# Staggering the seven products of gate and up blocks, a fourth pair of split tiles, and another order of the down products

## The chip, the core and the metric

The kernel runs on one core of a Trainium2 chip. The metric is device time in microseconds (us) of one execution. Of the engines this document speaks of five: PE (TensorE, the matmuls), DVE (VectorE), ACT (ScalarE), POOL (GpSimd) and SP (SyncE, which here only issues transfers). Each works through its own queue of instructions in the order that was fixed when the program was built.

## The reference: one layer of a hybrid decoder

The input is x, 512 tokens by 2048 features in float32. One layer has a mixing half (a gated linear recurrence and an RWKV-7 style state recurrence, side by side), a feed-forward half, a gated embedding, and a final RMS norm. The change touches the feed-forward half and the few steps ahead of it:

```python
h  = h + mixed @ w_out                      # output projection of the mixing half
hn = rmsnorm(h, ln_ffn)
g  = causal_dwconv(hn @ w_gate, conv_w, conv_b)   # 6144 columns, width 3
u  = hn @ w_up                              # 6144 columns
h  = h + (gelu(g) * u) @ w_down
```

All arithmetic has to be as good as float32. (The names of weights are shortened here.)

## The kernel before, in words

**Splits.** Each float32 operand A is split into hi, a copy rounded to the format that PE multiplies fast, and lo = A - hi. A product is then three matmuls, hi by hi, hi by lo and lo by hi. ACT makes hi (line L130) and DVE makes lo (L131), 128x1024 elements at a time for weights. The split weights lie in three rotating pairs of tiles, `whi` and `wlo` (HL = 3); the function `wfill` takes the next items of one long list (`ffn_items`, in the order in which PE uses them) and starts their splits up to LOOK = 2 units ahead. An item is either raw weights to be loaded by SP (L123) or a function that makes a sum of weight blocks.

**Projection and first forms.** For m = 0 to 15 PE computes 128 features of the output projection, DVE adds them to the residual `hT[m]` (L1243), and `forms(m)` makes split operands (L143 to L147 in a helper): from m below 8 for two of the seven products, from m of 8 and above for the other five. ACT squares `hT[m]` and POOL adds the squares up into `acc` (L1251), from which the norm's factor is later worked out (L189 to L202).

**Gate and up.** 48 blocks, gate and up in turn, each 256 columns by all 2048 features, as a two by two scheme that needs seven products instead of eight: q5, p1, p4, p6, p7, p2, p3 in this order (block 0: p1, p4, p2, q5, p7, p6, p3). A product is 24 matmuls of 128x256 (L1264 to L1266, over 8 steps of k). Its weights are blocks of the weight matrix or sums of them: q5 takes g21 + g22, a DVE add (L1120); p6 adds one more block to the same tile with an accumulating transfer that POOL issues (L1132), and p3 yet another one in the same way; p7 takes g21 + g11, a DVE add in place (L1130); p1, p4 and p2 take blocks as they are. DVE combines the results (L1289 to L1295); a gate block then goes through the convolution (L1305 to L1311), an up block is multiplied with it (L1354), and every second pair of blocks is written to memory together with four differences of its parts (`spill`).

**Down.** Eleven chunks of 512 hidden features in four groups of 3, 3, 3 and 2, each group for two halves of columns b, which gives eight passes. A pass runs products i = 0 to 6 one after the other, each over the chunks of the group; one chunk of one product is a unit of 12 matmuls of 128x512 (L1369 to L1371). Operands: i = 0 takes d0 loaded as it is; i = 1 takes d0 + d1, a DVE add into a tile of its own (L1150, tiles s24 to s26; d1 lies in s21 to s23); i = 2 and i = 6 add one block each to that tile by accumulating transfers from POOL (L1158); i = 3 takes a load; i = 4 adds it to d1 in place (L1156); i = 5 takes raw weights. The hidden operands are loaded into tiles "tmp", which three buffers share, and split (`hidden`).

**What sets the order.** A scheduler orders the program by priorities and a model of costs, and fixes each engine's queue. `wfill` runs at raised priority. On a queue, an instruction that waits holds up all that stand behind it.

After the down stage the last chunk, transposes, the gated embedding and the final norm follow; they use "tmp" too.

Of the kernel before, what the change touches and what calls it, by code (L numbers as in the profile page):

```python
# [5 lines left out]
F32R = mybir.dt.float32r  # L6
# [5 lines left out]
D = 2048  # L12
# [11 lines left out]
GROUPS = [(0, 3), (3, 6), (6, 9), (9, 11)]  # L24
KORDER = [(0, 1, 4, 5, 2, 3, 6, 7), range(8)]
# [63 lines left out]
class Builder:  # L89
# [22 lines left out]
    def wfill_(self):  # L112
        nc = self.nc
        while self.wn < len(self.wq) and len(self.wt) < self.LOOK:
# [9 lines left out]
            if own:  # L124
# [979 lines left out]
    def gate_order(self, p, w):  # L1104
# [3 lines left out]
    def gate_unit(self, p, w, u):  # L1108
        nc, par = self.nc, 4 * (w % 2)
        src = lambda i, j: self.A["wgu"][2 * p + i, w, j]  # L1110
        buf = lambda n: self.t(self.bp, "x%d" % (par + n), (128, 8, 128), bufs=1)

        def load(n, i, j):
            t = buf(n)
            nc.sync.dma_start(t, src(i, j))
            return t
        first = p + w == 0
        if u == "q5":
            self.g21, self.g22, self.gs = load(0, 1, 0), load(1, 1, 1), buf(3)
            nc.vector.tensor_tensor(self.gs, self.g21, self.g22, ALU.add)  # L1120
            return self.gs
        if u == "p1":
            self.g11 = load(2, 0, 0)
            return self.g11
        if u == "p4":
            return self.g22
        if u == "p7":
            if first:
                self.g11 = load(2, 0, 0)
            nc.vector.tensor_tensor(self.g21, self.g21, self.g11, ALU.add)  # L1130
            return self.g21
        nc.gpsimd.dma_start(self.gs, src(0, 0 if u == "p6" else 1), accum_op=ALU.add)  # L1132
        return self.gs


    def down_unit(self, ch, c, b, i):
# [24 lines left out]
    def ffn_items(self):  # L1161
# [4 lines left out]
        for p in range(NF // 2):  # L1166
            for w in range(2):
                for o in self.gate_order(p, w):
                    if o == "p2" or p + w == 0 and o in direct:
                        i, j = direct[o]  # L1170
                        r.append((A["wgu"][2 * p + i, w, j], u))
                    else:
                        r.append((lambda p=p, w=w, o=o: self.gate_unit(p, w, o), u))
# [22 lines left out]
    def phase2(self):  # L1196
# [7 lines left out]
        acc = T("acc")  # L1204
# [475 lines left out]
```

## Time and profile before

| what | us |
|---|---|
| median of 3 runs (lowest, highest) | 2728.83 (2725.93, 2731.3) |
| the profiled execution, its span | 2718.62, 2716.5 |
| PE busy | 2584.5 (95%) |
| DVE busy | 1901.9 (70%) |
| ACT busy | 1241.8 (46%) |
| POOL busy | 254.6 (9%) |
| mixing half, to about | 840 |
| projection and first forms | 840 to 908 |
| gate and up, 48 blocks | 908 to 1953.6 |
| down, eight passes | 1953.6 to 2440 |
| the rest | 2440 to 2716.5 |

The profile shows one execution. PE's busy share counts matmuls from their start to a modelled end, so that a PE at 95% can still lose time between matmuls; what a stage loses is better seen from its length against the number of its matmuls times the spacing of undisturbed ones. A row of a timeline has start, duration, engine, line, operation, tiles out and in, and in brackets how long the engine stood idle before it and what ended that. A row of waits has the total, the count and the longest.

### The profile page before, as it was taken

The page shows a single profiled execution, that of the slowest core. Times are in us where ns is not written, and L with a number is a line of the kernel's source. Part 1 is how long each engine was busy: PE and PEld are TensorE (multiplying, and loading weights), DVE is VectorE, ACT ScalarE, POOL GpSimd, SP SyncE. Part 2 cuts the span into 40 slices and gives each one's busy share as a digit, 9 for nine tenths or more (in the row PEclk, how much of TensorE's full clock was granted, in tenths as well). Part 3 has the DMA queues.
Part 4 walks back from the last instruction along what each step waited for, and adds up shares of the span by engine and source line. Part 5 has one row for each costly group of instructions (what it writes and reads, how often), then busy time and mean ns, then how long its engine had stood idle before and what let it go on. Part 6 is the DMA issues. An engine that isn't in the chain of part 4 may idle for free.

```text
span 2716.5 us, 51689 instructions
## 1 busy us (share of the span) xinstructions
PE 2584.5 (95%) x21922; PEld 2257.1 (83%) x21922; DVE 1901.9 (70%) x2594; ACT 1241.8 (46%) x1743; POOL 254.6 (9%) x268
## 2 busy tenths in 40 slices
PE   9989999999999899999999999999989989999997
PEld 8867777777777799999999999999967777777887
DVE  5765776666758887777777777777766676796447
ACT  6463556545525544343444334344555343435335
POOL 0010001001222200000000000000000000000001
PEclk9989999999999899999999999999999999999999
DMA  7212222122334565666566565666677676853233
GB/s 251 90 59 72 84 82 75 60 87 87 117 107 142 173 180 162 184 176 171 153 186 177 167 187 149 172 175 182 184 198 221 154 210 156 225 147 109 93 97 105
DMA packets 131448, 394.29 MB, mean 145 GB/s; under 512 B 14480, under 2 KB 26640, under 8 KB 131216
## 3 DMA queue, kind: packets, MB, share of 16 engines
q1 hardware_dynamic: 111056, 317.58, 33.6%
q0 software_dynamic: 20160, 73.41, 16.2%
q8 instruction: 171, 2.80, 0.4%
q14 instruction: 61, 0.50, 0.1%
HBM read 354.49 MB, written 36.44 MB: 144 GB/s over the span
## 4 chain that ended last, share of the span: by engine, by line
issue 21%; PE 19%; DMA 17%; DVE 11%; ACT 3%; POOL 2%; POOLq 0%; ACTq 0%; DVEq 0%; SPq 0%
DMA x<-wgu 16%; DVE wlo L131 5%; ACT whi L130 2%; PE mm L1266 2%; PE mm L1475 2%; PE mm L1477 2%; PE mm L1476 2%; PE mm L1264 2%; PE mm L1265 2%; POOL s L1158 1%; PE mm L1370 1%; PE mm L1371 1%; PE mm L1369 1%; PE wk L1264 1%; PE wk L1265 1%
## 5 line engine op out<-in xcount | busy, mean ns | idle before, releaser
L1266 PE MATMUL mm<-s,wlo 128*128 128x256 f32 x1920 | 552.7, 288 | 35.8 <-DVE wlo L131 35.2
L130 ACT ACTIVATE whi<-x 128x1024 fp32r<-128x1024 f32 x330 | 337.3, 1053 | 528.9 <-DMA x<-wgu 254.2
L1264 PE MATMUL mm<-s,whi 128*128 128x256 f32 x1920 | 548.1, 285 | 11.0 <-ACT whi L130 9.2
L131 DVE TENSOR_TENSOR wlo<-x,whi 128x1024 fp32r<-128x1024 f32 x330 | 401.7, 1221 | 210.0 <-ACT whi L130 209.2
L1265 PE MATMUL mm<-s,whi 128*128 128x256 f32 x1920 | 546.0, 284 | 0.2 <-DVE s L144 0.2
L131 DVE TENSOR_TENSOR wlo<-wraw,whi 128x1024 fp32r<-128x1024 f32 (+1 forms) x241 | 293.0, 1216 | 196.8 <-ACT whi L130 195.2
L130 ACT ACTIVATE whi<-wraw 128x1024 fp32r<-128x1024 f32 (+1 forms) x241 | 245.7, 1020 | 372.1 <-PE mm L162 187.1
L1266 PEld LDWEIGHTS mm<-s,wlo 128*128 128x128 f32 x1920 | 370.5, 193 | 48.1 <-DVE wlo L131 47.9
L1264 PEld LDWEIGHTS mm<-s,whi 128*128 128x128 f32 x1920 | 370.8, 193 | 14.3 <-ACT whi L130 12.2
L1265 PEld LDWEIGHTS mm<-s,whi 128*128 128x128 f32 x1920 | 370.7, 193 | 0.5 <-DVE s L144 0.4
L160 PE MATMUL mm<-x,whi 128*128 128x512 f32 x832 | 333.1, 400 | 0.9 <-DVE hT L450 0.9
L164 PE MATMUL mm<-x,wlo 128*128 128x512 f32 x832 | 332.8, 400 | 0.0
L162 PE MATMUL mm<-x,whi 128*128 128x512 f32 x832 | 331.2, 398 | 0.0
L1370 PE MATMUL mm<-wlo,s 128*128 128x512 f32 x680 | 274.1, 403 | 20.2 <-DVE wlo L131 20.1
L1369 PE MATMUL mm<-whi,s 128*128 128x512 f32 x680 | 272.7, 401 | 19.6 <-ACT whi L130 19.5
L1371 PE MATMUL mm<-whi,s 128*128 128x512 f32 x680 | 270.7, 398 | 0.0
L1266 PE MATMUL wk<-s,wlo 128*128 128x256 f32 x768 | 218.2, 284 | 0.8 <-DVE wlo L131 0.8
L1264 PE MATMUL wk<-s,whi 128*128 128x256 f32 x768 | 218.1, 284 | 0.0
L1265 PE MATMUL wk<-s,whi 128*128 128x256 f32 x768 | 217.9, 284 | 0.0
L160 PEld LDWEIGHTS mm<-x,whi 128*128 128x128 f32 x832 | 157.7, 189 | 36.4 <-issue 3.0
L162 PEld LDWEIGHTS mm<-x,whi 128*128 128x128 f32 x832 | 157.6, 189 | 33.7 <-issue 1.8
L164 PEld LDWEIGHTS mm<-x,wlo 128*128 128x128 f32 x832 | 157.3, 189 | 33.9 <-issue 1.9
(524 smaller groups left out, 4521.2 us busy)
## 6 DMA issues: line engine op xcount, KB each, us to landing
x<-wgu SPq DMA_DIRECT2D x144, 512.0 KB, 5.7
x<-wgu POOLq DMA_DIRECT2D x96, 512.0 KB, 5.5
wraw<-wz SPq DMA_DIRECT2D x80, 512.0 KB, 3.5
wraw<-wgu SPq DMA_DIRECT2D x50, 512.0 KB, 5.7
x<-wd SPq DMA_DIRECT2D x44, 512.0 KB, 4.3
s<-wd POOLq DMA_DIRECT2D x44, 512.0 KB, 6.0
wraw<-wpg SPq DMA_DIRECT2D x31, 512.0 KB, 3.5
wraw<-wd SPq DMA_DIRECT2D x30, 512.0 KB, 4.4
```

The costliest lines, as they stand in the source:

```text
L130: nc.scalar.activation(hi, raw, AF.Copy)
L131: nc.vector.tensor_tensor(lo, raw, hi.bitcast(F32), ALU.subtract)
L160: nc.tensor.matmul(ps, hi[:, k, :], xh, start=first and i == 0, stop=False)
L162: nc.tensor.matmul(ps, hi[:, k, :], xl, start=False, stop=False)
L164: nc.tensor.matmul(ps, lo[:, k, :], xh, start=False, stop=last and i == n - 1)
L1264: TE.matmul(ps, wh[:, k, :], xh, start=k == 0, stop=False)
L1265: TE.matmul(ps, wh[:, k, :], xl, start=False, stop=False)
L1266: TE.matmul(ps, wl[:, k, :], xh, start=False, stop=k == 7)
L1369: TE.matmul(ps, x[0][:, k, ts_], w[0][:, k, :], start=first and k == 0, stop=False)
L1370: TE.matmul(ps, x[0][:, k, ts_], w[1][:, k, :], start=False, stop=False)
L1371: TE.matmul(ps, x[1][:, k, ts_], w[0][:, k, :], start=False, stop=last and k == 1)
L1475: TE.matmul(pg[tt], xh[:, ts_], wh[:, i, :], start=first and u + i == 0, stop=False)
```

## The change: what it does

1. **Gate order.** `gate_order` is now one list over all 48 blocks. Block n runs q5, then p3 of block n-1, then p1, p4, p6, p7, p2 of its own; p3 of the last block comes at the end. Block 0 runs p1, p4, p2, q5, p7, p6. The state of a block is kept in a dictionary, because two blocks are open at a time.
2. **Fourth pair.** Every fourth weight split (k % 4 == 3) goes into tiles x12 and x15 instead of the three rotating pairs, and LOOK is 3. The working tiles of a block that lay in x15 move into two buffers "fm", the outputs of up blocks use two tiles (x10, x11) instead of three.
3. **p6 of blocks 0 and 47** is summed by a DVE add instead of an accumulating transfer.
4. **Down order** is 1, 0, 2, 3, 6, 4, 5; the load of d0 is made with product 1, and the hidden operands are prepared in the same order.
5. **First forms.** For m of 8 and above the intermediate sums are formed with one DVE and one ACT instruction less, and DVE instead of POOL adds the squares up. `acc` lies in another pool.
6. **"tmp"** has two buffers instead of three.

```diff
+ORDER = (1, 0, 2, 3, 6, 4, 5)
...
-            if own:
+            if len(own) == 2:
+                hi, lo = (self.t(self.bp, n, shape, F32R, bufs=1) for n in own)
+            elif own:
...
-        return ("p1", "p4", "p2", "q5", "p7", "p6", "p3") if p + w == 0 else ("q5", "p1", "p4", "p6", "p7", "p2", "p3")
+        o = [(0, u) for u in ("p1", "p4", "p2", "q5", "p7", "p6")]
+        for n in range(1, NF):
+            o += [(n, "q5"), (n - 1, "p3")] + [(n, u) for u in ("p1", "p4", "p6", "p7", "p2")]
+        return o + [(NF - 1, "p3")]
...
-        nc.gpsimd.dma_start(self.gs, src(0, 0 if u == "p6" else 1), accum_op=ALU.add)
-        return self.gs
+        if u == "p6" and n in (0, NF - 1):
+            nc.vector.tensor_tensor(g["s"], g["s"], g[11], ALU.add)
+        else:
+            nc.gpsimd.dma_start(g["s"], src(0, 0 if u == "p6" else 1), accum_op=ALU.add)
+        return g["s"]
...
         if i == 0:
-            self.d0[c] = load(plain(), 0, 0)
             return self.d0[c]
         if i == 1:
-            self.d1[c], self.dq[c] = load(buf(21 + c), 0, 1), buf(24 + c)
+            self.d0[c], self.d1[c], self.dq[c] = load(plain(), 0, 0), load(buf(21 + c), 0, 1), buf(24 + c)
             nc.vector.tensor_tensor(self.dq[c], self.d0[c], self.d1[c], ALU.add)
...
+        for k, (n, o) in enumerate(self.gate_order()):
+            own = (("x12", "x15") if k % 4 == 3 else ())
...
-                for i in range(7):
+                for i in ORDER:
...
+        self.LOOK = 3
...
-            f1 = T("tmp", 3, (128, 2, 256))
-            differ(f1[:, 0], k)
+            f1 = T("fm", 2, (128, 2, 256))
             if m < 8:
+                V.tensor_tensor(f1[:, 0], b, a, ALU.subtract)
...
-            SC.activation(f1[:, 0], f1[:, 0], AF.Copy, scale=g0)
-            SC.activation(f1[:, 1], halves(hT[k])[1], AF.Copy, scale=g0)
-            V.scalar_tensor_tensor(f2[:, 0], b, g, f1[:, 0], ALU.mult, ALU.subtract)
+            SC.activation(f1[:, 0], b0, AF.Copy, scale=g0)
+            V.scalar_tensor_tensor(f1[:, 1], b, g, f1[:, 0], ALU.mult, ALU.subtract)
+            V.scalar_tensor_tensor(f2[:, 0], a0, g0, f1[:, 1], ALU.mult, ALU.add)
             V.scalar_tensor_tensor(f2[:, 1], a, g, f2[:, 0], ALU.mult, ALU.subtract)
-            V.scalar_tensor_tensor(f3[:, 0], b, g, f1[:, 1], ALU.mult, ALU.subtract)
...
-                sq = T("tmp", 3)
+                sq = T("tmp", 2)
                 SC.activation(sq, hT[m], AF.Square)
-                G.tensor_tensor(acc, acc, sq, ALU.add)
+                (G if m < 8 else V).tensor_tensor(acc, acc, sq, ALU.add)
...
-                hids[ch, i] = hidden(src, 3 * i + ch - lo)
+                hids[ch, i] = hidden(src, 3 * ORDER.index(i) + ch - lo)
...
-            for i in range(7):
+            for j, i in enumerate(ORDER):
```

How the queues move, first **DVE in a steady stretch of the gate stage**, before. The rows from the split of p3 of one block on (`wlo` from x3) to the next block's combination; L131 with a `wlo` is a lo, x3 or x7 holds the sum for q5, p6 and p3 of even or odd blocks.

```order
L1289 TENSOR_TENSOR x15_1916_13642<-wk_1925_13732,x15_1916_13642 128x256
L1290 SCALAR_TENSOR_TENSOR x15_1916_13642<-mm_1917_13643,x15_1916_13642 128x256
L131 TENSOR_TENSOR wlo_1931_13768<-x3_1906_13568,whi_1930_13767 128x1024
L1120 TENSOR_TENSOR x3_1961_14032<-x0_1959_14028,x1_1960_14030 128x1024
L1292 TENSOR_TENSOR x15_1916_13642<-x15_1916_13642,wk_1929_13765 128x256
L1130 TENSOR_TENSOR x0_1959_14028<-x0_1959_14028,x2_1964_14062 128x1024
L131 TENSOR_TENSOR wlo_1937_13805<-x7_1935_13802,whi_1936_13804 128x1024
L1293 TENSOR_TENSOR x8_1914_13640<-mm_1917_13643,x15_1916_13642 128x512
L131 TENSOR_TENSOR wlo_1940_13835<-x6_1938_13832,whi_1939_13834 128x1024
L1295 TENSOR_TENSOR x8_1914_13640<-mm_1932_13797,x15_1916_13642 128x512
```

The same stretch after the change; there the lines are L134 (lo), L1127 (add for q5), L1137 (add for p7) and L1294 to L1300 (combination), and x15 as a target is the lo of the fourth pair.

```order
L134 TENSOR_TENSOR wlo_1931_13699<-wraw_1929_13696,whi_1930_13698 128x1024
...
L134 TENSOR_TENSOR wlo_1937_13734<-x7_1935_13731,whi_1936_13733 128x1024
L1294 TENSOR_TENSOR fm_1917_13593<-wk_1932_13726,fm_1916_13592 128x256
L1295 SCALAR_TENSOR_TENSOR fm_1916_13592<-mm_1919_13595,fm_1917_13593 128x256
L134 TENSOR_TENSOR x15_1940_13766<-x3_1906_13497,x12_1939_13765 128x1024
L1127 TENSOR_TENSOR x3_1963_13963<-x0_1961_13959,x1_1962_13961 128x1024
L1297 TENSOR_TENSOR fm_1917_13593<-fm_1917_13593,wk_1938_13763 128x256
L1137 TENSOR_TENSOR x0_1961_13959<-x0_1961_13959,x2_1970_14028 128x1024
L134 TENSOR_TENSOR wlo_1944_13799<-x6_1942_13796,whi_1943_13798 128x1024
L1298 TENSOR_TENSOR x8_1918_13594<-mm_1919_13595,fm_1917_13593 128x512
```

Before, p3's lo (from x3) stands ahead of both adds of the next block and of its q5's lo (from x7). After, q5's lo of the next block (from x7) stands ahead of p3's lo (from x3), and the add for a q5 that stands behind it (L1127) is that of the block after the next one, into x3 again.

**DVE at the boundary of two down passes**, before: lo's of products 5 (from `wraw`) and 6 (s24 to s26), and the adds L1150 for the next pass.

```order
L131 TENSOR_TENSOR wlo_3178_23215<-wraw_3176_23212,whi_3177_23214 128x1024
L131 TENSOR_TENSOR wlo_3180_23232<-s24_3128_22942,whi_3179_23231 128x1024
L1150 TENSOR_TENSOR s24_3199_23345<-x0_3187_23285,s21_3198_23343 128x1024
L131 TENSOR_TENSOR wlo_3182_23249<-s25_3132_22962,whi_3181_23248 128x1024
...
L1150 TENSOR_TENSOR s25_3203_23365<-x1_3190_23303,s22_3202_23363 128x1024
L131 TENSOR_TENSOR wlo_3186_23270<-s26_3138_22986,whi_3185_23269 128x1024
...
L1150 TENSOR_TENSOR s26_3215_23404<-x2_3195_23325,s23_3214_23402 128x1024
L131 TENSOR_TENSOR wlo_3189_23288<-x0_3187_23285,whi_3188_23287 128x1024
L131 TENSOR_TENSOR wlo_3192_23306<-x1_3190_23303,whi_3191_23305 128x1024
```

After, where L1159 is that add and the lo's are those of products 4 (s21 to s23) and 5 (`wraw`):

```order
L134 TENSOR_TENSOR wlo_3209_23186<-s21_3151_22881,whi_3208_23185 128x1024
L134 TENSOR_TENSOR wlo_3211_23203<-s22_3156_22903,whi_3210_23202 128x1024
...
L1159 TENSOR_TENSOR s24_3229_23301<-x0_3227_23297,s21_3228_23299 128x1024
L134 TENSOR_TENSOR wlo_3213_23220<-s23_3161_22925,whi_3212_23219 128x1024
L1159 TENSOR_TENSOR s25_3234_23323<-x1_3232_23319,s22_3233_23321 128x1024
L134 TENSOR_TENSOR wlo_3218_23242<-wraw_3216_23239,whi_3217_23241 128x1024
L1159 TENSOR_TENSOR s26_3239_23345<-x2_3237_23341,s23_3238_23343 128x1024
L134 TENSOR_TENSOR wlo_3221_23260<-wraw_3219_23257,whi_3220_23259 128x1024
...
L134 TENSOR_TENSOR wlo_3224_23278<-wraw_3222_23275,whi_3223_23277 128x1024
L134 TENSOR_TENSOR wlo_3231_23304<-s24_3229_23301,whi_3230_23303 128x1024
```

Before, the adds stood among the lo's of product 6 and behind them came the lo's of the next pass's product 0, from plain loads x0 and x1. After, they stand among the lo's of products 4 and 5, write s24 to s26 from loads into s21 to s23, which product 4's splits just read, and the first lo's of the next pass are those of the sums.

**DVE from the gate's end into the first down pass**, before:

```order
L1292 TENSOR_TENSOR x15_2859_21670<-x15_2859_21670,wk_2902_21868 128x256
L131 TENSOR_TENSOR wlo_2914_21919<-x0_2912_21916,whi_2913_21918 128x1024
...
L1293 TENSOR_TENSOR x12_2858_21669<-mm_2860_21671,x15_2859_21670 128x512
L131 TENSOR_TENSOR wlo_2923_21964<-x1_2921_21961,whi_2922_21963 128x1024
...
L1150 TENSOR_TENSOR s24_2944_22031<-x0_2912_21916,s21_2943_22029 128x1024
...
L131 TENSOR_TENSOR wlo_2942_22014<-x2_2940_22011,whi_2941_22013 128x1024
L1150 TENSOR_TENSOR s25_2948_22051<-x1_2921_21961,s22_2947_22049 128x1024
L131 TENSOR_TENSOR wlo_2946_22034<-s24_2944_22031,whi_2945_22033 128x1024
```

After:

```order
L1295 SCALAR_TENSOR_TENSOR fm_2896_21658<-mm_2899_21661,fm_2897_21659 128x256
L1297 TENSOR_TENSOR fm_2897_21659<-fm_2897_21659,wk_2944_21897 128x256
L1298 TENSOR_TENSOR x11_2898_21660<-mm_2899_21661,fm_2897_21659 128x512
...
L1159 TENSOR_TENSOR s24_2947_21902<-x0_2945_21898,s21_2946_21900 128x1024
L1300 TENSOR_TENSOR x11_2898_21660<-mm_2956_21949,fm_2896_21658 128x512
L1159 TENSOR_TENSOR s25_2959_21954<-x1_2957_21950,s22_2958_21952 128x1024
L134 TENSOR_TENSOR wlo_2949_21905<-s24_2947_21902,whi_2948_21904 128x1024
L1159 TENSOR_TENSOR s26_2970_22003<-x2_2968_21999,s23_2969_22001 128x1024
L134 TENSOR_TENSOR wlo_2961_21957<-s25_2959_21954,whi_2960_21956 128x1024
```

Before, lo's from plain loads (x0, x1, x2) stand first and the adds between and behind them. After, two adds stand ahead of the first lo of the down stage, with the last combinations of block 47 (L1297 to L1300) in between.

More of the change, by code (lines that the diff above doesn't have):

```diff
@@ L1304, in conv @@
+            if u == "p3":
+                V.tensor_tensor(two(out[:, 0]), two(g["up"]), fm, ALU.add)
+            if n == 0 and u == "q5":
+                rt = self.tok_rstd(acc, D, RMS_EPS, k2)
+            if n == 0 and u == "p6":
+                self.rstd_bcast(acc, D, RMS_EPS, k2, rs, rt)
+            if n == NF - 1:
+                for i in {"q5": (0,), "p1": (1,), "p4": (2, 3), "p6": (4,), "p7": (5,), "p2": (6,)}.get(u, ()):
+                    group_form(0, ORDER[i])
         def conv(p, z, c):
@@ L1451, in phase2 @@
         for k in range(2):
[L1452 removed]
+            r = T("tmp", 2)
             nc.sync.dma_start(r, A["pT"][k])
```

160 lines of the change are left out of this document (74 added, 86 removed).

## The prediction, made before the changed kernel ran

> **What bounds the kernel now.** I read three views in this order: the windows by stage (how much of each stage TensorE, PE, loses), the chain of waits inside the lossy stages, and the timelines of the engines in that chain. First the windows; the columns are the window, its length, busy time and count of instructions of PE, PE's weight loads, DVE, ACT and POOL, then granted clock, DMA share and GB/s.
>
> ```profile
> 840.00:925.00 85.00, 78.86 (x364) 66.08 (x362) 81.41 (x132) 54.08 (x105) 23.47 (x15) 0.96 0.54 183
> 908.13:949.16 41.03, 30.81 (x185) 28.90 (x184) 29.88 (x43) 16.91 (x29) 9.94 (x7) 0.79 0.72 205
> 949.16:1009.64 60.48, 60.48 (x506) 60.48 (x505) 49.47 (x57) 29.23 (x31) 5.25 (x6) 1.00 0.59 161
> 1009.64:1953.60 943.96, 905.92 (x7395) 891.25 (x7394) 703.98 (x793) 384.25 (x425) 76.34 (x87) 1.00 0.62 173
> 1953.60:2027.30 73.70, 63.12 (x255) 48.56 (x254) 48.33 (x49) 36.30 (x49) 5.27 (x6) 0.95 0.75 219
> 2027.30:2440.00 412.70, 383.50 (x1612) 306.23 (x1611) 298.23 (x325) 178.12 (x209) 33.34 (x38) 0.98 0.69 185
> ```
>
> Gate blocks 1 to 3 (third row) take 60.48 us with PE never idle: 20.16 us a block of 168 matmuls, the floor. Block 0 (41.03 us) loses 20.9. The other 44 blocks need 44 x 20.16 = 887.0 and take 943.96: **56.9 us lost**. No engine is full there: DVE is busy 704 of 944 us, so what bounds is a chain. This is one turn of it:
>
> ```profile
> 1397.60 5.41 DMA x<-wgu
> 1403.05 2.77 issue
> 1405.84 6.85 DMA x<-wgu
> 1412.80 1.07 ACT whi L130
> 1413.89 1.24 DVE wlo L131
> 1415.19 1.11 issue
> 1416.29 0.41 DVE x L1292
> 1416.78 0.98 issue
> 1417.76 1.23 DVE wlo L131
> ...
> 1393.36 1.23 DVE L1120 TENSOR_TENSOR x<-x,x 128x1024 f32<-128x1024 f32 x1
> 1394.84 1.22 DVE L1130 TENSOR_TENSOR x<-x,x 128x1024 f32<-128x1024 f32 x1
> ```
>
> The accumulating transfer for p6 starts when q5's lo is out, its sum is split (the first "issue", 2.77), the transfer for p3 follows, p3 is split, and in DVE's queue p3's lo stands before the next block's L1120, L1292, L1130 and the lo of the next q5 (the last two rows show the two adds that the chain calls "issue", in the turn before). That lo starts the next p6. The turn is 5.41 + 2.77 + 6.85 + 1.07 + 1.24 + 1.11 + 0.41 + 0.98 + 1.23 and small gaps, 21.4 us against 20.16.
>
> The down stage has 154 units of 12 matmuls. The first two PE rows below are 23 matmuls apart, 0.227 us each, so 2.72 a unit and 8.17 a product of three chunks; 154 units need 419.4 us and take 73.7 + 412.7 = 486.4: **67.0 lost**. Nearly all of it stands at product i=2, whose operand is the sum of product 1 with one block of weights added by an accumulating transfer, three of them per product:
>
> ```profile
> 2169.72 0.39 PE L1369 MATMUL mm<-whi,s 128*128 128x512 f32 x1
> 2174.94 0.39 PE L1371 MATMUL mm<-whi,s 128*128 128x512 f32 x1
> 2178.52 0.50 PE L1369 MATMUL mm<-whi,s 128*128 128x512 f32 x1 [3.19 <-ACT whi L130]
> 2179.78 0.50 PE L1370 MATMUL mm<-wlo,s 128*128 128x512 f32 x1 [0.76 <-DVE wlo L131]
> 2180.97 0.63 PE L1371 MATMUL mm<-whi,s 128*128 128x512 f32 x1
> 2181.39 0.63 PE L1369 MATMUL mm<-whi,s 128*128 128x512 f32 x1
> ...
> 2162.86 0.89 POOL L1158 DMA_DIRECT2D s<-wd  x1 [30.76 <-DVE wlo L131]
> 2169.11 0.87 POOL L1158 DMA_DIRECT2D s<-wd  x1 [5.36 <-DVE s L144]
> 2177.62 0.89 POOL L1158 DMA_DIRECT2D s<-wd  x1 [7.64 <-issue]
> 2183.31 0.88 POOL L1158 DMA_DIRECT2D s<-wd  x1 [4.80 <-issue]
> 2197.62 0.87 POOL L1158 DMA_DIRECT2D s<-wd  x1 [7.50 <-DVE x L1386]
> ...
> 2231.64 0.88 POOL L1158 DMA_DIRECT2D s<-wd  x1 [33.15 <-DVE wlo L131]
> 2264.51 0.88 POOL L1158 DMA_DIRECT2D s<-wd  x1 [8.56 <-issue]
> ```
>
> Six accumulating transfers a pass (three for i=2, three for i=6) go one at a time: the six starts span 2162.86 to 2197.62, 6.95 us apart, in the next pass 2231.64 to 2264.51, 6.57 apart, 5.7 where nothing else interferes (2177.62 to 2183.31). The third start came 8.5 us after the second, and PE stood 3.19 us for that operand. Behind the gap matmuls start 0.42 apart instead of 0.227: the clock is halved for some 3.4 us, which costs about 1.7 more.
>
> The Trainium skill, "TensorE: Matmul & The Clock Gate", Part 1: The HAM clock gate, says the array falls to half clock after at least one idle window of about 3.4 us. By that, gaps below 3.4 would cost only themselves, and rival 2 below would come out 13.6 lower. The trace has the clock fall behind a gap of 3.19, so the figure is about right; for shorter gaps I keep the dearer price.
>
> **The change, part by part.** All against the profiled execution (2718.62 us, 2.1 around its span), which lies 10.2 under the median of the runs shown, 2728.83; I take savings off the median.
>
> *Gate order and fourth pair.* Work is the same count of matmuls, splits and transfers. p3 of block n moves behind q5 of block n+1, so p6 and p3 each get a product (2.88 us) more, and the lo of q5 stands ahead of p3's lo in DVE's queue: the turn above is cut open, since nothing of block n+1's q5 now waits for block n's p3. Every fourth split has a pair of its own, so a split can begin three products (8.64 us) ahead of use instead of two (5.76). From q5's lo to p3's use there is now more than a block; the chain needs 5.41 + 2.77 + 6.85 + 1.07 + 1.24 = 17.3. What remains is DVE, 704/44 = 16.0 us a block of 20.16. I expect 20.3 a block: 0.14 x 44 = 6 us lost, **51 saved** (bounds: 0.45 a block left, 37 saved; none left, 57).
>
> *Block 0 and the first forms.* The first two rows give a line's count, its shortest, median and longest duration in ns, and its first and last start.
>
> ```profile
> L147 DVE SCALAR_TENSOR_TENSOR s<-hT,par,s x22: 472/480/1526, 847.3 to 915.7; 128x256 fp32r<-128x256 f32 x22
> L1251 POOL TENSOR_TENSOR acc<-acc,tmp x10: 1420/1831/1841, 867.8 to 927.2; 128x512 f32<-128x512 f32 x10
> ...
> 904.91 0.41 DVE L1216 TENSOR_TENSOR tmp<-hT 128x256 f32<-128x256 f32 x1
> 911.01 0.41 DVE L1216 TENSOR_TENSOR tmp<-hT 128x256 f32<-128x256 f32 x1
> ```
>
> From 840 to 925 DVE is full (81.41 of 85) and one m takes it 6.1 us (904.91 to 911.01), PE 24 x 0.227 = 5.45. L147 takes 1.52 instead of 0.48 while POOL's square-sum runs. For m from 8 the change drops L1216 (0.35 in the queue), the slowed L147 (1.04), and adds the square-sum on DVE (about 0.6, as a 128x512 add): 5.3 an m, below PE. Over seven m's the forms end some 4.5 us sooner. Block 0 lost 41.03 - 30.81 = 10.2 in gaps and 41.03 x 0.21 = 8.6 by halved clock. The order p1, p4, p2, q5, p7, p6 starts with loads of raw weights, and p6 is summed on DVE (1.2 us where a transfer took 5.4). I expect 12 lost: **9 saved** (0 if the gap and its clock come back at another product, 16 if only the norm's own matmuls stay).
>
> *Down order 1, 0, 2, 3, 6, 4, 5.* Product 0 now lies between 1 and 2, so i=2 is used 16.3 us after product 1 starts, not 8.17. With the first transfer at -0.5 us (the rows give -1.4 and +0.2 against product 1) and starts x apart, the third has landed and is split at -0.5 + 3x + 2.3 = 21.0 for x = 6.4, needed at 21.8: the 50 us at i=2 go. What is late next: i=6 now follows 3, and its last chunk is used at 38.1, ready at 1.8 + 6x, that is 40.2 for x = 6.4 (between 5.7 and 6.95): 2.1 late in six passes; the two-chunk passes, ready 1.8 + 4x, needed 24.5, are 2.9 late. Sum 44x - 263.2 = 18.4.
>
> At the boundary of passes product 1 comes first, so the sum of the next pass stands in DVE's queue between the lo's of products 4 and 5 and waits for a load into the buffer that product 4's split has only just released:
>
> ```profile
> L1142 SPq DMA_DIRECT2D s<-wd x20: 327/332/422, 1953.3 to 2380.8; - x20
> DMA to landing us min/median/max: 3.3/6.0/8.6
> ...
> 1961.80 0.52 PE L1370 MATMUL mm<-wlo,s 128*128 128x512 f32 x1 [2.37 <-DVE wlo L131]
> 2211.18 0.50 PE L1369 MATMUL mm<-whi,s 128*128 128x512 f32 x1 [1.17 <-ACT whi L130]
> ```
>
> A pair is free when 6's first chunk ends, 5.4 us before product 4 starts, so the split of 4's first chunk (2.3) ends some 3 us before it; with a landing 3.3 to 8.6 later, the adds (1.22 each) and the lo's queued behind them make 5's operands 0 to 4 us late; the same place costs 0 to 2.5 now (second PE row, 1.17 + 0.76 + clock). I take 2 at seven boundaries, 14. At the gate's end product 1 needs buffers that the last p2 and p3 hold, a load (6.0) and an add: 6 to 9 us idle where the trace has 2.37 and its clock, 4.2 in all; I take 8.7. Down then loses 18.4 + 14 + 8.7 = 41: **26 saved**. Look-ahead 3 brings nothing here, there are still three pairs. Bounds: x = 5.7 and free boundaries, loss 12, 55 saved; x = 6.95 with a halved clock in every pass, 42.6 + 13.6 + 22.7 = 79, 12 lost.
>
> *Two "tmp" buffers instead of three.*
>
> ```profile
> PE wk L1433 <- DVE s L147: 2.0, 1, 2.0
> tmp<-pT SPq DMA_DIRECT2D x2, 256.0 KB, 3.2
> ```
>
> In the tail a second small load now waits for the first's split: at most one landing, 3.2, where PE already waits 2.0; the rest of the tail has PE waiting 1.2 in all. **2 lost** (0 to 5).
>
> Sum: 51 + 9 + 26 - 2 = 84, so 2728.8 - 84 = **2645 us**, 2635 on the profile's scale.
>
> **The rivals.**
> 1. *Down nearly free* (x = 5.7, boundaries hidden): 51 + 9 + 55 - 2 = 113, **2616**. For it: 5.7 stands between two starts, and a transfer of the same size landed in 5.41 in the gate's chain. Against: 6.95 and 6.57 on average.
> 2. *Serial transfers take over* (x = 6.95): the wait at i=2 moves whole to i=6, 51 + 9 - 12 - 2 = 46, **2683**. For it: that is the pace shown. Against: in those rows some starts waited for DVE, not for the queue.
> 3. *The gate order doesn't do what it says*: the rotating pairs and DVE's order still tie p3 to q5, 20.7 a block, so 0.54 x 44 = 24 lost and 33 saved instead of 51, in all 66: **2663**. For it: DVE's 16 of 20.16 us in strict order. Against: blocks 1 to 3 run at the floor with the old order as long as the chain has not caught up.
> 4. *Slower*: down's six transfers collide with the loads that now come earlier (x and s of the next pass), at x = 9, near the longest gaps between starts above (8.5, and 8.56 + 0.88 = 9.4 ahead of the last row). Loss 44 x 9 - 263.2 + 13.6 + 22.7 = 169, 102 more than now; with 51 + 9 - 2 = 58 gained, 44 slower: **2773**. It decides from x = 8.0, where loss reaches 67 + 58 = 125. Against: a mean over six starts above 7 is in neither pass shown.
>
> The Trainium skill, "DMA: Bandwidth & Descriptors", Issuing engines are not separate DMA queues, says that transfers of all engines end on the same 16 engines and interleave. That would make any load that now falls beside an accumulating transfer lengthen it, which speaks for rivals 2 and 4; the trace shows starts 5.7 and 8.5 us apart in one pass, and no row here proves that the loads beside them are the cause.
>
> **How the numbers follow.** Forecast 0.45, rival 1 0.20, rival 2 0.20, rival 3 0.10, rival 4 0.05. About 0.2% (5.5 us) is what a measurement of this kernel can tell from no change. Only rival 4 ends above it, and a mix of 2 and 3 could end within: faster 0.93, same 0.02, slower 0.05. The range 2608 to 2690 holds the forecast and rivals 1 to 3 with some slack for unsharp terms. The forecast's own range is 2628 to 2662.
>
> **What would show it.** Right: gate blocks of 20.16 to 20.4 us from block 4 on, no L1266 wait on q5's or p3's lo, PE clock 1.00 there; block 0 near 32; in down no gap at the third product run (i=2), small gaps at i=6's last chunk and at 5; the first down pass starting with a gap of 6 to 9 us. Wrong: gate blocks still near 21, gaps over 3 us at each i=6 with POOL starts 7 apart, or DVE adds of the next pass with idle time ahead that PE shares.

## The result: 2638 us, and where the time went

The changed kernel takes 2638.39 us (median, 2635.63 to 2647.67) against 2727.38 for the kernel before (2722.37 to 2731.3). The ratio is 0.9681, 95% interval 0.9651 to 0.9710. A second series of it, beside later experiments, gave 2638.21 against 2721.8, ratio 0.9696 (0.9681 to 0.9711). The forecast was 2645 in a range of 2608 to 2690.

The profiled execution has a span of 2634.4 us against 2716.5. First the windows of the changed kernel (window, length, busy time and count of PE, PE's weight loads, DVE, ACT, POOL, granted clock, DMA share, GB/s): block 0, blocks 1 to 47, the down stage.

```profile
900.60:931.40 30.80, 25.97 (x186) 24.86 (x186) 24.56 (x36) 13.45 (x22) 3.00 (x3) 0.89 0.67 219
931.40:1879.00 947.60, 947.60 (x7898) 947.50 (x7896) 765.46 (x851) 422.74 (x454) 81.75 (x92) 1.00 0.69 183
1879.10:2353.50 474.40, 441.80 (x1850) 350.88 (x1849) 344.09 (x367) 214.23 (x257) 39.13 (x44) 0.98 0.71 191
```

In blocks 1 to 47 PE is busy for the whole 947.60 us, and 47 x 20.16 = 947.5: the gate stage is at its floor. Block 0 fell from 41.03 to 30.80, with 4.8 us of gaps instead of 10.2 and a granted clock of 0.89 instead of 0.79. The down stage needs 419.4 and takes 474.4, so 55 us are still lost there. The largest part of the chain that ended last is now PE's own work (first row of that view, shares of the span, before and after):

```profile
issue 21%; PE 19%; DMA 17%; DVE 11%; ACT 3%; POOL 2%; POOLq 0%; ACTq 0%; DVEq 0%; SPq 0%
```

```profile
PE 47%; issue 16%; DVE 5%; POOL 2%; ACT 2%; DMA 1%; POOLq 0%; ACTq 0%; DVEq 0%
```

Transfers had 17% of this chain before and have 1% now. By stage, with the second profile of the changed kernel beside the first (lengths in us; the projection counts from its first matmul, down from the gate's last matmul to the last one of its last unit):

| stage | before | after | after, second profile | saved | predicted |
|---|---|---|---|---|---|
| mixing half (not changed) | 842.7 | 835.3 | 838.7 | 7.5 and 4.0 | 0 |
| projection | 65.4 | 65.4 | 65.4 | 0 | 0 |
| gate block 0 | 41.0 | 30.7 | 30.7 | 10.3 | 9 |
| blocks 1 to 47 | 1004.3 | 947.6 | 948.0 | 56.7 and 56.3 | 51 |
| down | 484.2 | 474.4 | 467.2 | 9.8 and 17.0 | 26 |
| the rest | 278.8 | 281.0 | 282.7 | -2.2 and -3.9 | -2 |

The first row is a warning: the same code in front of the change took 835.3 to 843.3 us over the thirteen profiles of this study that have the changed first stages or variants of them, so a difference of some us between two whole spans says nothing, and stages have to be compared. The changed parts account for 75 to 80 us of the 82 to 84 between the profiles. (The medians lie 89 apart.)

### The profile page after: what moved, and what is told of

It is laid out like the page before. It is cut to its first block, busy times and chain, and to the rows that moved or that the text cites. A ratio compares the mean times of both kernels' runs of the same rounds, so it can differ in the third digit from the quotient of the medians.

```text
span 2634.4 us, 51652 instructions
## 1 busy us (share of the span) xinstructions
PE 2550.1 (97%) x21922; PEld 2239.9 (85%) x21922; DVE 1909.8 (72%) x2596; ACT 1248.7 (47%) x1735; POOL 238.9 (9%) x258
## 4 chain that ended last, share of the span: by engine, by line
PE 47%; issue 16%; DVE 5%; POOL 2%; ACT 2%; DMA 1%; POOLq 0%; ACTq 0%; DVEq 0%
PE mm L1271 9%; PE mm L1269 9%; PE mm L1270 9%; PE wk L1269 4%; PE wk L1270 4%; PE wk L1271 4%; PE mm L1483 2%; PE mm L1485 2%; PE mm L1484 2%; POOL s L1167 1%; DVE wlo L134 1%; PE mm L163 1%; PE mm L165 1%; PE mm L167 1%; DVE s L150 1%
## 5 line engine op out<-in xcount | busy, mean ns | idle before, releaser
L133 ACT ACTIVATE whi<-x 128x1024 fp32r<-128x1024 f32 x258 | 272.3, 1059 | 371.6 <-PE mm L1270 225.1
L133 ACT ACTIVATE whi<-wraw 128x1024 fp32r<-128x1024 f32 (+1 forms) x229 | 233.0, 1017 | 378.8 <-PE mm L165 182.2
L1269 PE MATMUL mm<-s,whi 128*128 128x256 f32 x1432 | 405.3, 283 | 2.6 <-ACT s L146 2.6
L1271 PE MATMUL mm<-s,wlo 128*128 128x256 f32 x1432 | 405.5, 283 | 1.1 <-DVE wlo L134 1.1
L1270 PE MATMUL mm<-s,whi 128*128 128x256 f32 x1432 | 405.6, 283 | 0.6 <-DVE s L147 0.6
L134 DVE TENSOR_TENSOR wlo<-x,whi 128x1024 fp32r<-128x1024 f32 x258 | 314.9, 1222 | 104.0 <-ACT whi L133 97.2
L134 DVE TENSOR_TENSOR wlo<-wraw,whi 128x1024 fp32r<-128x1024 f32 (+1 forms) x229 | 278.9, 1218 | 139.5 <-ACT whi L133 138.0
L1269 PEld LDWEIGHTS mm<-s,whi 128*128 128x128 f32 x1432 | 274.9, 192 | 2.9 <-ACT s L146 2.8
L1271 PEld LDWEIGHTS mm<-s,wlo 128*128 128x128 f32 x1432 | 275.1, 192 | 1.3 <-DVE wlo L134 1.3
L1270 PEld LDWEIGHTS mm<-s,whi 128*128 128x128 f32 x1432 | 275.0, 192 | 0.9 <-DVE s L147 0.8
L1378 PEld LDWEIGHTS mm<-wlo,s 128*128 128x128 f32 x680 | 129.9, 191 | 60.4 <-DVE wlo L134 34.1
L1377 PEld LDWEIGHTS mm<-whi,s 128*128 128x128 f32 x680 | 129.9, 191 | 43.7 <-ACT whi L133 16.7
L1269 PE MATMUL wk<-s,whi 128*128 128x256 f32 x584 | 166.1, 284 | 0.0
```

The lines of the kernel that those rows point to most:

```text
L133: nc.scalar.activation(hi, raw, AF.Copy)
L134: nc.vector.tensor_tensor(lo, raw, hi.bitcast(F32), ALU.subtract)
L1269: TE.matmul(ps, wh[:, k, :], xh, start=k == 0, stop=False)
L1270: TE.matmul(ps, wh[:, k, :], xl, start=False, stop=False)
L1271: TE.matmul(ps, wl[:, k, :], xh, start=False, stop=k == 7)
L1377: TE.matmul(ps, x[0][:, k, ts_], w[0][:, k, :], start=first and k == 0, stop=False)
```

## The experiments

All start from the changed kernel; a time is a median, and a ratio stands against the kernel before on the same chip.

### Gate: the order or the fourth pair?

`e1_no_pair` drops the fourth pair:

```diff
-            own = (("x12", "x15") if k % 4 == 3 else ())
+            own = ()
```

> The changed kernel without the fourth pair of split tiles (every split uses the three rotating pairs; the staggered order, the look-ahead of 3 and all else stay). Theory 'order': the staggered order alone cuts the turn in which p3's lo stood ahead of the next q5's lo, so gate blocks stay at 20.2 to 20.4 us and the time is 2638 to 2650. Rival 'pair': the gain comes from splits beginning a product earlier, gate blocks go back towards 21.1 us, 45 us more, 2680.

Measured 2642.76 us, ratio 0.9705 (0.9675 to 0.9734), not told apart from 0.9681. `e2_no_stagger` keeps the pair and puts each block's products in one piece again:

```diff
-            o += [(n, "q5"), (n - 1, "p3")] + [(n, u) for u in ("p1", "p4", "p6", "p7", "p2")]
-        return o + [(NF - 1, "p3")]
+            o += [(n, u) for u in ("q5", "p1", "p4", "p6", "p7", "p2", "p3")]
+        return o
```

> The changed kernel with each block's seven products in one piece again (q5, p1, p4, p6, p7, p2, p3; block 0 ends with p3), but with the fourth pair and the look-ahead of 3. Theory 'order': p3's lo is again ahead of the next q5's lo, the turn of 21.4 us closes again, blocks at about 21.1, 2675 to 2685. Rival 'pair': the fourth pair lets q5 be split early enough, blocks at 20.2 to 20.4, 2638 to 2650.

Measured 2674.56 us, ratio 0.9833 (0.9800 to 0.9866). The windows of blocks 1 to 47, first without the pair, then without the stagger:

```profile
939.00:1886.50 947.50, 947.50 (x7898) 947.48 (x7896) 772.31 (x849) 423.96 (x455) 80.72 (x92) 1.00 0.68 182
```

```profile
936.30:1916.70 980.40, 962.33 (x7898) 952.00 (x7896) 743.90 (x847) 398.55 (x451) 81.61 (x92) 1.00 0.63 175
```

Without the pair the gate stands at its floor, 947.50. Without the stagger it takes 980.40, 20.86 a block, with 33 of the 57 us lost again. (The profiled execution of this kernel is the slowest of its four, 2686.97 us; by the medians it lies 36 us over the changed one.) In the chain of waits of that kernel the old turn is back (start, length, what; the two DMA rows are the accumulating transfers of p6 and p3, L134 is a lo, L1294 and L1137 are DVE operations of the neighbouring block):

```profile
1498.39 5.50 DMA x<-wgu
1503.93 2.78 issue
1506.73 7.40 DMA x<-wgu
1514.23 1.07 ACT whi L133
1515.32 1.24 DVE wlo L134
1516.62 1.11 issue
1517.73 0.41 DVE fm L1294
1518.14 1.13 DVE x L1137
1519.27 1.15 DVE x L134
1520.46 0.38 PE mm L1271
```

Row by row it is the chain of before: transfer, split, transfer, p3's split, the next block's adds, q5's lo, PE. So the order cuts the turn, and the pair adds nothing to the steady gate once the order is there. With the old order a block takes 20.86 here against 21.37 in the kernel before (1004.3 by 47). The two kernels differ by the pair, by LOOK 3 and by the working tiles, and no run tells which of these gave the half us. Theory "order" holds; its figure of 21.1 was a little too dear. Both runs keep LOOK at 3, so what the order is worth with LOOK 2 is not shown.

### First forms: who adds up the squares?

`e6_acc_pool` gives all sixteen square-sums back to POOL:

```diff
-                (G if m < 8 else V).tensor_tensor(acc, acc, sq, ALU.add)
+                G.tensor_tensor(acc, acc, sq, ALU.add)
```

> The changed kernel with the square-sum of the first stage on POOL for all sixteen m. Before, a step of this stage took DVE 6.1 us; after, gate starts 7.5 us earlier. Theory: POOL's adds slow L147's successor from 0.48 to 1.52 us, one per m (1.04 more against 0.6 saved), so the gate starts 3 to 4 us later and block 0 loses 0 to 3 more: 2640 to 2645. Rival: the two dropped instructions made the gain, POOL's adds cost nothing: within 1 us of 2638.

Measured 2647.12 us, above both ranges expected. The ratio is 0.9719 (0.9692 to 0.9745), against 0.9696 (0.9681 to 0.9711): the intervals overlap, but the stages tell. DVE's add into the residual, which comes once an m, in the changed kernel and then with POOL's adds:

```profile
877.31 0.68 DVE L1248 TENSOR_TENSOR hT<-hT,mm 128x512 f32<-128x512 f32 x1
882.75 0.68 DVE L1248 TENSOR_TENSOR hT<-hT,mm 128x512 f32<-128x512 f32 x1
```

```profile
880.38 0.68 DVE L1248 TENSOR_TENSOR hT<-hT,mm 128x512 f32<-128x512 f32 x1
886.32 0.68 DVE L1248 TENSOR_TENSOR hT<-hT,mm 128x512 f32<-128x512 f32 x1
```

An m takes 5.44 us in the changed kernel, PE's own 24 x 0.227 = 5.45, 5.94 with POOL's adds, 6.10 before. So POOL's adds cost DVE 0.5 an m. Against the expectation the gate starts no later (the projection is 65.4 us long in all kernels, as PE waits for no form there); the loss is in block 0, 33.9 us instead of 30.7, and 0.9 in the blocks behind. In all the other kernels with DVE's adds block 0 takes 30.6 to 32.5.

### Down: what is the order worth?

`e3_old_down` has the products in the order 0 to 6 again:

```diff
-ORDER = (1, 0, 2, 3, 6, 4, 5)
+ORDER = (0, 1, 2, 3, 4, 5, 6)
```

(with the load of d0 back at product 0).

> The changed kernel with the down products in the order 0 to 6 and the load of d0 at product 0 again. The traces have 67 us lost in down before and 55 after. Theory: the order is worth this 12 us, the stalls of 6 to 7 us at product 2 come back, those at product 6 and the long first gap go: 2645 to 2655. Rival: what product 2 gains product 6 gives back, the order is worth nothing: 2635 to 2642.

Measured 2653.95 us, ratio 0.9751 (0.9724 to 0.9779): the order is worth some 15 us by the medians and 19 to 26 by the length of the stage in the profiled execution, the slowest of its four. From here on, what PE loses at a product is the time from the last matmul of the product before it to its own last matmul, less 0.227 us for each of its matmuls. In this trace the stalls at product 2 are back (50.3 us in all, 5.1 to 7.7 a pass), and down takes 493.1 us, more than the 484.2 of the kernel before: products 4 and 5 lose 8 and 12 us, where they lost 3 and 6. Why the old order does worse here than in the kernel before (two "tmp" buffers are one difference) was not tried.

`e4_order_146` and `e5_order_32` try two other orders, `(1, 0, 2, 3, 4, 6, 5)` and `(1, 0, 3, 2, 4, 6, 5)`:

> The changed kernel with the down order 1, 0, 2, 3, 4, 6, 5: product 6 comes one product (8.17 us) later, product 4 one earlier. In the trace of the changed kernel products 6 lose 25 us in all and products 2 lose 14. Theory 'serial transfers': the six accumulating transfers go one at a time and are 2 to 6 us late at 6; with 8.17 more the 25 us go, and the sums of the next pass no longer wait for a load: 2610 to 2620. Rival 'engine queues': the lo's of product 6 are late because DVE and ACT are held by other work, which only moves: 2632 to 2642.

> The changed kernel with the down order 1, 0, 3, 2, 4, 6, 5: products 2 and 6 each come one product later. Theory 'serial transfers': the losses at both (14 and 25 us) go, a few us at the first pass stay: 2600 to 2612. Rival 'reload': product 3 now follows product 0 directly, its load into the tile that 0's split has just released lands 4 to 7 us later and 3 becomes late by 2 to 4 us a pass: 2620 to 2640.

Measured 2632.84 us, ratio 0.9671 (0.9637 to 0.9705), for the first, and 2648.77, ratio 0.9727 (0.9699 to 0.9755), for the second. In the first, product 6 loses 2.9 us instead of 25, as "serial transfers" has it, but 8.9 appear at product 4, which now has the place where 6 was, and products 1 and 0 lose 19 where they lost 13: part of the loss moved, and the time is not told from the changed kernel's, as "engine queues" had it. In the second the reload is late as its rival has it (11.7 us at product 3), and product 6 loses 11.0 again, since its transfers can start only after the later product 2. Neither theory had the size of this one.

### Down: what makes product 6 late?

In the changed kernel's second pass of group 1 POOL issues six accumulating transfers:

```profile
2076.86 0.88 POOL L1167 DMA_DIRECT2D s<-wd  x1 [27.53 <-DVE wlo L134]
2082.86 0.88 POOL L1167 DMA_DIRECT2D s<-wd  x1 [5.12 <-issue]
2092.32 0.90 POOL L1167 DMA_DIRECT2D s<-wd  x1 [8.59 <-issue]
...
2113.06 0.89 POOL L1167 DMA_DIRECT2D s<-wd  x1 [7.77 <-issue]
```

The time to landing of the one issued at 2082.86 alone, from the view by tile:

```profile
DMA to landing us min/median/max: 9.1/9.1/9.1
```

They start 7.24 us apart ((2113.06 - 2076.86) / 5), and the second took 9.1 us to land. PE loses 5.8 us at product 6 there. `e8_no_prep` leaves out the preparation of the next groups' hidden operands, `e9_no_prep_loads` leaves out only its loads and splits one tile again and again:

```diff
             for ch in range(lo, hi):
+                if g > 0:
+                    hids[ch, i] = hids[ch - 3, i]      # e8
+                    continue
...
+                if g > 0:                               # e9
+                    if i == ORDER[0] and ch == lo:
+                        once[g] = T("fm", 2, (128, 2, 256))
+                        nc.sync.dma_start(once[g], src)
+                    t = T("s%d" % (3 * ORDER.index(i) + ch - lo), 1, (128, 2, 2, 256), F32R)
+                    self.split(t[:, 0], t[:, 1], once[g])
```

> The changed kernel without preparing the hidden operands of groups 1 to 3: they reuse those of the group before, so 18 to 21 loads and as many splits fall out of each second pass, and the result is not the reference's. In the changed kernel product 6 loses 4.5, 5.8 and 5.7 us in the passes that prepare the next group, and 0, 0 and 2.9 in those that don't. Theories 'loads' and 'splits' both expect these 16 us to go: about 2620. Theory 'serial transfers alone' expects the accumulating transfers to stay as far apart, and 2635 to 2640.

> As the kernel without preparation, but the splits of the hidden operands of groups 1 to 3 are made, all from one tile that is loaded once per group; only their loads fall out (again not the reference's result). Theory 'loads' (they lengthen the accumulating transfers beside them): the stalls at product 6 go as there, about 2620, and the starts of POOL's transfers in those passes come 6.0 to 6.5 us apart instead of 7.2 to 7.5. Theory 'splits' (ACT and DVE are held): the stalls stay, 2633 to 2640.

Measured 2625.04 us, ratio 0.9638 (0.9609 to 0.9667), and 2623.35, ratio 0.9630 (0.9599 to 0.9661); down takes 455.1 and 458.3 us. The same pass without the loads, splits kept:

```profile
2072.31 0.88 POOL L1167 DMA_DIRECT2D s<-wd  x1 [26.67 <-DVE wlo L134]
...
2103.09 0.89 POOL L1167 DMA_DIRECT2D s<-wd  x1 [4.77 <-DVE s L147]
```

Now they start 6.16 us apart ((2103.09 - 2072.31) / 5), and product 6 loses nothing. As the two kernels gain alike, the 13 to 15 us are due to the loads and not to the splits. But this pass is the exception. Theory "loads" said that the stalls at product 6 would go, and over the whole stage they stay, as what PE loses at each product shows (us, whole stage):

| product | changed kernel | its second profile | e8, no preparation | e9, splits kept |
|---|---|---|---|---|
| 1 | 6.2 | 5.5 | 5.2 | 6.5 |
| 0 | 7.0 | 4.8 | 0.4 | 1.3 |
| 2 | 14.1 | 15.0 | 6.4 | 12.8 |
| 6 | 25.3 | 18.8 | 20.5 | 17.3 |
| 3, 4 and 5 | 2.6 | 3.8 | 3.4 | 1.2 |

In both kernels the loss at product 0 goes, in `e8` also half of that at product 2; at product 6 they lose about as much as the second profile of the changed kernel. The starts don't tell them from it either: in the three passes that prepare a next group they are 7.5, 7.2 and 7.5 apart in the changed kernel, 6.8, 7.5 and 6.0 in its second profile, and 7.1, 6.2 and 7.2 without the loads. The loads of x for products 3 and 1, of 512 KB each, run beside these transfers too and were left in. So the time came out near the 2620 of the theory, but by another way than it says.

What goes with the loads is a wait of ACT. The prepared operands are loaded into "tmp", and their splits (L146) stand in ACT's queue among those of the weights (L133). ACT's waits for these loads in the down stage (total, count, longest), in the changed kernel and then without the preparing loads:

```profile
ACT s L146 <- DMA tmp<-rd: 51.3, 28, 6.2
ACT s L146 <- DMA tmp<-dd: 48.2, 20, 5.3
```

```profile
ACT s L146 <- DMA tmp<-dd: 10.6, 3, 4.2
ACT s L146 <- DMA tmp<-rd: 8.0, 5, 3.0
```

In the kernel before, with three "tmp" buffers, they were 15.3 (dd) and 13.0 us (rd). The first pass of group 1 in the changed kernel shows how this makes product 0 late (4.0 us lost there): its splits (`whi` from x) come out of ACT only behind such a wait, and PE waits for the first of them.

```profile
2023.64 0.63 ACT L146 ACTIVATE s<-tmp 128x512 fp32r<-128x512 f32 x1 [3.06 <-DMA tmp<-rd]
2024.17 2.94 ACT L133 ACTIVATE whi<-x 128x1024 fp32r<-128x1024 f32 x3
...
2025.27 0.49 PE L1377 MATMUL mm<-whi,s 128*128 128x512 f32 x1 [1.07 <-ACT whi L133]
```

How much of the 13 to 15 us is ACT's waiting and how much the longer transfers was not separated, and the changed kernel with three "tmp" buffers was not tried.

### Down without accumulating transfers

`e10_add6` sums product 6 with an SP load and a DVE add, `e11_add26` products 2 and 6; `e12_add6_146` is `e10` with the order 1, 0, 2, 3, 4, 6, 5:

```diff
+        if i == 6:              # e10, e12; always in e11
+            r = self.t(self.cp, "wraw", (128, 2, 512), bufs=self.RAW)
+            nc.sync.dma_start(r, src(1, 1 if i == 2 else 0))
+            nc.vector.tensor_tensor(self.dq[c], self.dq[c], r, ALU.add)
+            return self.dq[c]
```

> The changed kernel with product 6 of down summed otherwise: SP loads the block into one of the two tiles for raw weights and DVE adds it (1.22 us), in place of POOL's accumulating transfer. Theory 'serial transfers': three of six transfers leave POOL's queue, the 25 us at product 6 go, three DVE adds of 1.22 a pass fit beside (DVE is busy 297 of 404 us there): 2612 to 2622. Rival 'engine queues': 6 is late because of DVE's and ACT's own work, and more of it makes no gain: 2632 to 2645.

> As the kernel with product 6 added by DVE, but product 2 as well, so no accumulating transfer is left in down. Theory 'serial transfers': 14 us at product 2 go too, six adds a pass (7.3 us of 57): 2600 to 2612. Rival 'two raw tiles': their loads and the adds stand in line with product 5's, the loads come late and DVE's queue stands on them: 2625 to 2645.

> Product 6 added by DVE, and the order 1, 0, 2, 3, 4, 6, 5. In that order alone products 6 still lost 3 us and products 4 some 9 in the trace. Theory 'serial transfers': the 25 us at 6 are gone by either step, together they are worth little more than one: 2608 to 2620. Rival 'engine queues': no gain over the changed kernel, 2630 to 2645.

> The changed kernel once more, unchanged, beside these three on the same chip: 2633 to 2645 by every theory.

| kernel | us | ratio (95%) | down, us |
|---|---|---|---|
| changed kernel again | 2638.21 | 0.9696 (0.9681 to 0.9711) | 467.2 |
| e10: 6 by DVE | 2632.39 | 0.9674 (0.9661 to 0.9687) | 470.1 |
| e12: 6 by DVE, other order | 2631.98 | 0.9670 (0.9657 to 0.9684) | 468.4 |
| e11: 2 and 6 by DVE | 2619.18 | 0.9621 (0.9607 to 0.9635) | 454.8 |

With 6 alone taken off POOL, its loss falls to 3.6 us, but products 0 and 3 lose 12 us each where they lost 7 and 1 (5 and 2 in the second profile): the gain is at most 6 us and not sure. "Serial transfers" misses the three times: `e10` and `e12` lie where "engine queues" had them, `e11` between the theory and its rival. With all six off POOL the kernel is 19 us faster than the changed one, outside both intervals: **2619 us is the best of the study**. The waits of PE in its down stage (total, count, longest), the window of that stage, and DVE's queue in the last pass:

```profile
PE mm L1382 <- DVE s L1399: 7.2, 1, 7.2
PE mm L1383 <- DVE wlo L134: 4.7, 8, 1.8
```

```profile
1887.90:2342.80 454.90, 435.22 (x1858) 349.76 (x1857) 394.35 (x415) 216.97 (x257) 0.00 (x0) 0.98 0.61 200
```

```profile
2311.86 2.35 DVE L1407 TENSOR_TENSOR x<-x,x 128x1024 f32<-128x1024 f32 x2
2314.13 1.21 DVE L134 TENSOR_TENSOR wlo<-s,whi 128x1024 fp32r<-128x1024 f32 x1
2315.27 2.35 DVE L1407 TENSOR_TENSOR x<-x,x 128x1024 f32<-128x1024 f32 x2
2317.54 1.27 DVE L1399 TENSOR_TENSOR s<-s,mm 128x512 f32<-128x512 f32 x2
```

DVE is busy 394 of 455 us there, and what is late next is its own queue: in the last pass the combinations of the other half (L1407) stand ahead of the add that empties PE's accumulators (L1399), and PE waits 7.2 us for it.

## Why the prediction was right, and which terms were off

**Gate, 51 forecast, 56.5 measured.** The step "the turn above is cut open" is shown from both sides, by the floor without the pair and by the turn that came back without the stagger. The 6 us kept for DVE's load did not appear: PE never waits between blocks 3 and 47 with DVE at 765 of 948 us. The step that gave a share to the fourth pair ("a split can begin three products ahead") was not needed.

**Block 0, 9 forecast, 10.3 measured.** The step "5.3 an m, below PE" gave what the adds into the residual show, an m as long as PE's 5.45. That the gain would appear in block 0 and not in the projection is as forecast, by the expectation of the experiment on POOL it was not. That experiment accounts for 3.2 of the 10.3; how the rest divides among the order of block 0, the DVE sum of p6 and the shorter first forms was not tried.

**Down, 26 forecast, 10 and 17 measured.** The mechanism was right: the 50 us at product 2 went, and 6 became the next to be late. Three of its terms were mis-sized.

- At product 2 the forecast was 0 ("ready 21.0, needed 21.8"); measured are 14.1 and 15.0 us. The transfers are not all of it. In the pass shown, product 2's first chunk waits for this, on DVE, on PE, and in the list of what L1165 waited for over the stage:

```profile
2093.52 1.23 DVE L1165 TENSOR_TENSOR s<-s,x 128x1024 f32<-128x1024 f32 x1 [3.48 <-DMA x<-wd]
2094.66 1.22 DVE L134 TENSOR_TENSOR wlo<-s,whi 128x1024 fp32r<-128x1024 f32 x1
```

```profile
2095.94 0.50 PE L1378 MATMUL mm<-wlo,s 128*128 128x512 f32 x1 [1.22 <-DVE wlo L134]
```

```profile
  DMA x<-wd: 20.7, 13
```

  L1165 is the add for product 4, two to three products before its use. It waits 3.48 us for product 3's load, and product 2's lo stands behind it. Over the stage these adds sit idle for that load for 20.7 us (last row, total and count); in the kernel without accumulating transfers it is 4.9. The queue rows of the forecast looked only at the boundary of passes. That moving this add alone would free product 2 was not tried.
- At product 6 the forecast was 18.4 for starts 6.4 apart; measured are 25.3 and 18.8. The mean start of a pass lies between 6.4 and 7.5 in the first profile and between 6.0 and 7.5 in the second: one number for all passes was the mistake. The rest of the term held: with each pass's own x in the forecast's 1.8 + 6x and 1.8 + 4x, less what the pass had already lost ahead of product 6, the sum comes to 25 and 17. (For the kernels without the pair and with POOL's adds the same sum falls 8 and 10 short of the 23 and 22 measured.)
- The boundary of passes was forecast at 14 and gave 9 and 7 (stalls at products 4, 5, 1 and 0), but not where the forecast had them: at product 5 lie 1.6 and 1.1, at product 0 7.0 and 4.8, the largest of these behind ACT's wait shown above; the gate's end at 8.7 and gave 5.5 and 5.1.

**The rest, 2 lost forecast, 2 and 4 in the two profiles.** Of the thirteen profiles with two "tmp" buffers eight have 280.5 to 283.0 us there and five 277.6 to 279.4, as the single one before (278.8), so this loss is not established. The forecast looked for the price of two buffers in this stage alone; in down ACT's waits for loads into them went from 28 to 99.5 us, which no term held.

**Of the rivals,** "serial transfers" (2683) was half of what happened in down, and its price fell on a gate that did better than forecast. The argument held against it, that some starts waited for DVE and not for the queue, was a misreading: in the profile before, every start that follows another in its pass comes 0.31 us after that one has landed, also where the row names DVE. "The gate order doesn't do what it says" is refuted. "Slower" would have needed starts 8.0 apart; the highest mean of a pass in the changed kernel was 7.5. The bound of 12 us left in down at x = 5.7 does not follow from the forecast's own formula: 44x - 263.2 is negative there and the gate's end is 8.7, so that "down nearly free" should have read about 2613 instead of 2616.

**The sum.** That 2645 came within 7 us of the time is in part luck. The changed stages gave 75 to 80 us where the forecast had 84, since down fell 9 to 16 short and the gate (5.5) and block 0 (1) made up for 6.5 of it. The medians still fell by 89: 4 to 7.5 us of the rest appear in the unchanged mixing half of the profiled executions, and the profiled execution of the kernel before lies 9 us under its median, those of the changed kernel 2 and 3. No term held either.

## What to carry to other kernels

When PE waits at one point of a loop and no engine is full, write down one turn of the chain with its durations, and look for the instruction that ties the next round to this one by its place in a queue and not by data: putting it back in its old place brought 33 of 57 us of loss back here, where leaving out another buffer pair cost nothing. When a wait is moved, list for the new place every instruction that stands ahead of it on the in-order engine, adds made early for a later product too, since these take the transfer's lateness with them. Compare stages and not spans where the untouched part alone varies by 8 us. When an experiment is meant to remove a stall, look whether that stall went, and not only whether the time came out as forecast.

## What the runs showed of the hardware that was not expected

POOL's accumulating transfers go one at a time. In the fence on the changed kernel's pass the transfer issued at 2082.86 landed 9.1 us later, at about 2092.0, and the next was issued at 2092.32, though its idle time is put down to nothing that the profile shows ("issue"). It is so throughout: in the down stages before and after, 70 of the 72 issues that follow another in their pass come 0.31 or 0.32 us after that one's landing. SP's loads overlap in the same stretch. What varies is the landing: the transfer at 2076.86 took 5.7 us, with no load issued by SP while it ran, the next one 9.1 beside four, issued from 2083.28 to 2090.07. The Trainium skill, "DMA: Bandwidth & Descriptors", Issuing engines are not separate DMA queues, says that transfers of all engines interleave on the same 16 engines. These two landings agree with it; the kernel without the preparing loads does so only in the pass shown (starts 6.16 apart instead of 7.24).

The clock is halved after less than 3.4 us of idle time. Behind gaps of 1.32 and 0.76 us matmuls start 0.42 apart, behind the gap of 1.22 us ahead of 2095.94 they start 0.23 apart:

```profile
2120.74 0.50 PE L1377 MATMUL mm<-whi,s 128*128 128x512 f32 x1 [1.32 <-ACT whi L133]
2122.00 0.69 PE L1378 MATMUL mm<-wlo,s 128*128 128x512 f32 x1 [0.76 <-DVE wlo L134]
2122.92 0.63 PE L1377 MATMUL mm<-whi,s 128*128 128x512 f32 x1
2123.34 0.63 PE L1378 MATMUL mm<-wlo,s 128*128 128x512 f32 x1
...
2096.52 0.40 PE L1377 MATMUL mm<-whi,s 128*128 128x512 f32 x1
2096.75 0.40 PE L1378 MATMUL mm<-wlo,s 128*128 128x512 f32 x1
```

The windows around the two places (length, busy time of PE, ..., granted clock third from the end):

```profile
2118.70:2122.10 3.40, 1.32 (x6) 0.54 (x4) 2.07 (x3) 2.99 (x4) 0.00 (x0) 1.00 0.33 113
2122.10:2125.50 3.40, 3.40 (x9) 2.66 (x10) 3.12 (x4) 1.64 (x3) 0.00 (x0) 0.51 0.52 161
2094.80:2098.20 3.40, 2.26 (x10) 1.86 (x11) 3.40 (x5) 0.16 (x2) 0.00 (x0) 1.00 0.71 136
```

PE is idle for 2.1 of the 3.4 us ahead of the slow stretch, and for 1.1 of the 3.4 around the other gap. In the clock records of this profile the down stage has six slow stretches of 3.4 us each, and the 3.4 us ahead of each hold 1.8 to 2.7 us of idle PE, half of them or more. The Trainium skill, "TensorE: Matmul & The Clock Gate", Part 1: The HAM clock gate, gives one idle window of about 3.4 us as the condition; here some 2 us of idle time in two pieces was enough, so the measurement decides, and for gaps that add up to that the dearer price of the forecast was the right one.
